# Two layers of an SSM and attention encoder: output projection in blocks of 512 columns, transposes of B and C at a fixed place

## The chip, the cores and the metric

The kernel runs on one core of a Trainium2 chip. The time is that of one execution on the device in microseconds (us), the median of several runs. The engines are TensorE (PE, matmuls; its weight loads are shown as PEld), VectorE (DVE), ScalarE (ACT), GpSimd (POOL) and SyncE (SP), which issues most of the DMA transfers.

## What is computed

A token matrix x of 256 rows and 2,048 columns goes through two layers. Cut to what matters:

```python
for l in range(DEPTH):                       # DEPTH = 2
    u, gate_ssm, q, k, v, gate_attn = split(h @ w_in[l])     # 2048 -> 6 x 1024
    y = s5_scan(u, ..., reverse=False) + s5_scan(u, ..., reverse=True) + d * u
    y = gelu(y); y = y * sigmoid(y @ w_glu[l] + b_glu[l])
    y = y * silu(gate_ssm)
    o = rms_norm(diff_attention(q, k, v, lam)) * (1 - lam_init) * silu(gate_attn)
    h = layer_norm(alpha * h + concat(y, o) @ w_out[l], ln_g[l], ln_b[l])
```

Here s5_scan is a complex diagonal state space model (SSM) over 64 groups of 16 channels with 64 states, run in both directions over the 256 tokens; B (64 x 16 for a group) maps the inputs to states, C maps states to outputs. diff_attention is softmax attention with two maps for each of 8 heads. All of it is in float32.

## The kernel before, in words

**Three products.** PE multiplies rounded float32 (fp32r). To keep float32's accuracy each operand is split into a high and a low part, and `mm3` (L167 to L170) issues high x high, high x low and low x high into one accumulator. A weight piece of 512 rows x 256 columns (512 KB) comes by one DMA of SP into one of 4 `raw` buffers (`load`, L143); `do_split` (L155) makes `wh` by a cast on ACT (L162) and `wl` by a subtraction on DVE (L164), two pieces ahead of their use. `step` (L829) takes the next piece of the list `jobs`, issues its matmuls, prepares the pieces behind it and then lets side work in. Almost all of PE's time is in these projections.

**The list of jobs.** For each layer: the input projection in blocks of 256 columns (4 pieces of 512 rows each, 24 blocks); the output projection's rows of the attention half (8 blocks of 256 columns, 2 pieces each: the first half, L942 to L951, put into `part_r` with the residual `xr` added); the projection of the GLU (4 blocks); the output projection's rows of the SSM half (the second half, L976 on). The last blocks of the second half (`late`: the last two of eight in layer 0 and the last three in layer 1) are interleaved by token halves with the LayerNorm that follows (`ln_finish`, L214). In the output projection the tokens are the weights of PE: one matmul has 128 rows of the token matrix as 128x128 weights and 256 columns of w_out as its moving operand. A block has two accumulators, one for each half of the tokens, in one PSUM bank.

**Side work.** The SSM and the attention heads are generators that run in lanes: after each step `side` (L778) lets the lanes go on as far as a budget allows; a `yield c, n` says what the piece cost and in how many steps it may go on. Lanes that the change touches or that its effects reach: `ssm_load` (L403 on; B and C are loaded, and PE transposes them, L421 and L446, 16 each a layer, with copies on ACT), `ssm_in` (U, the input of the SSM, times B, from L473 on), `ssm_scan`, and `ssm_out` (eight outputs `o`; for each of them on ACT a copy of states `bh`, L638, of taps `kw`, L570, and `lt`, L582; on PE L577 and the matmuls L586, L596 and L601 into `ss`; then ACT's copy `ub<-ss`, L607; at the end L626 applies gelu to `yT`, the SSM's output read back from memory, with a load of ACT's function table).

**What sets the order.** The code gives an order by its text and lanes; a scheduler then orders the instructions of each engine by a modelled timeline, with the waits that the data need. `after(ins)` pins an instruction behind another of the same engine. PSUM has eight banks: `acc` 2, `sc` one tile of 2 banks (the heads' scores, and later an accumulator of late blocks), `tp` 2, `ss` 2. In SBUF the tag `a8` has three buffers of 8 KB a partition, which pass from one tensor to the next: B's and C's sources in `ssm_load`, U, the heads' output oT, the SSM gates `sgs` (Silu of four gate blocks, L934), yT and the token operand of the second half.

Of the kernel before, what the change touches and what calls it, by code (L numbers as in the profile page):

```python
# [38 lines left out]
SCAN_COST = 1.0  # L39
HEAD_HOPS = (1,1,2,2,2,3)  # L40


@with_exitstack
def kernel(
# [80 lines left out]
    for l in range(DEPTH):  # L125
        for s in range(4):
            jobs += [(l, "in", 0, s), (l, "in", 1, s)]
        order = [2, 3]
        for hp in range(4):
            order += [8 + hp, 12 + hp, 16 + hp]  # L130
        order += list(range(20, 24)) + list(range(4, 8))
        for cb in order:
            jobs += [(l, "in", cb, s) for s in range(4)]
        for cb in range(8):
            jobs += [(l, "out", cb, 2), (l, "out", cb, 3)]
        for cb in range(4):
            jobs += [(l, "glu", cb, 0), (l, "glu", cb, 1)]
        for cb in range(8):
            jobs += [(l, "out", cb, 0), (l, "out", cb, 1)]
    raws, split = {}, {}  # L140
    newest = [None]

    def load(i):  # L143
        if i >= len(jobs):
            return
        l, kind, cb, s = jobs[i]
        src = {"in": w_in, "glu": w_glu, "out": w_out}[kind][l]
        raw = T([128, KT, 256], "raw", RAW_BUFS)
        newest[0] = SY.dma_start(
            raw,  # L150
            src[s * KT * 128:(s + 1) * KT * 128, cb * 256:(cb + 1) * 256].rearrange("(k p) c -> p k c", p=128),
        ).ins
        raws[i] = raw

    def do_split(i, wh=None, wl=None, behind=None):  # L155
# [3 lines left out]
        if wh is None:  # L159
            wh = T([128, KT, 256], "wh", SPLIT_AHEAD + 1, F32R)  # L160
            wl = T([128, KT, 256], "wl", SPLIT_AHEAD + 1, F32R)
        A.copy(wh, raw)  # L162
# [4 lines left out]
    def mm3(o, lh, ll, rh, rl, first, last):  # L167
        PE.matmul(o, lhsT=lh, rhs=rh, start=first, stop=False, skip_group_check=True)  # L168
        PE.matmul(o, lhsT=lh, rhs=rl, start=False, stop=False, skip_group_check=True)  # L169
        PE.matmul(o, lhsT=ll, rhs=rh, start=False, stop=last, skip_group_check=True)  # L170

# [231 lines left out]
    def ssm_load(l):  # L403
# [14 lines left out]
        for q in range(4):  # L418
            t = tp_bank([128, 4, 128])
            for c in range(4):  # L420
                PE.transpose(t[:, c, :], natv[:, :, 4 * q + c], ident)  # L421
            A.copy(Bv[:, :, 4 * q:4 * q + 4], t.rearrange("p c g -> p g c"))
# [17 lines left out]
        Cv = z.C.rearrange("p r (o g) c -> p r o (g c)", o=8)  # L440
        yield 0.0, 1
        for ri in range(2):
            for q in range(2):
                t = tp_bank([128, 4, 128])
                for o in range(4):
                    PE.transpose(t[:, o, :], cn[:, ri, 4 * q + o, :], ident)  # L446
                A.mul(Cv[:, ri, 4 * q:4 * q + 4, :], t, 1.0 if ri == 0 else -1.0)
# [390 lines left out]
    def acc_bank():  # L838
        return PS([128, 2, 256], "acc", 2)

    def sub_step(acc, s, hi, lo, k0, k1, tok_major=False, budget=BUDGET, k_outer=False):

# [22 lines left out]
    for l in range(DEPTH):  # L865
# [76 lines left out]
        part_r = [T([128, D], tag) for tag in ("xh1", "xl1")]  # L942
        for cb in range(8):
            cs = slice(cb * 256, (cb + 1) * 256)
            xr = T([128, 2, 256], "xr", 2)
            SY.dma_start(xr, xres[:, cs].rearrange("(i p) d -> p i d", p=128))
            acc = acc_bank()
            for s in (0, 1):
                sub_step(acc, s, M.hi, M.lo, 0, 7, tok_major=True)
            for i in range(2):  # L950
                V.scalar_tensor_tensor(part_r[i][:, cs], xr[:, i], ALPHA, acc[:, i, :], mult, add)  # L951
        finish(l_out)
# [22 lines left out]
        late = range(7 - len(places), 8)  # L975
        for cb in range(late[0]):  # L976
            if l + 1 < DEPTH and cb in (0, 2):
                with after(newest[0]):
                    next(l_load)
            cs = slice(cb * 256, (cb + 1) * 256)  # L980
            acc = acc_bank()
# [95 lines left out]
```

## Time and profile before

| | us |
|---|---|
| median of three runs | 1003.33 |
| lowest and highest of them | 999.39, 1005.35 |
| the profiled execution | 1002.55 |
| its span in the trace | 1000.8 |
| PE busy | 955.8 |
| DVE busy | 780.3 |
| ACT busy | 576.0 |
| POOL busy | 71.7 |

The mean granted clock of PE over the span is 0.991. The page of the profile gives the busy time of each engine; the timeline gives the instructions of a stretch with their start and length, and in square brackets how long the engine was idle before one and what released it; the waits say who waited for whom; the windows give busy time, granted clock and the share of the DMA engines for a stretch. A matmul's length goes from its start to its modelled end, and matmuls overlap, so a matmul's share in PE's time is read from the distance between starts.

### The profile page before, as it was taken

Reading aid. Unit: us, or ns where it says so; the run is one execution under the profiler, and the core shown is the slowest. Engines: PE = TensorE matmul, PEld = TensorE weight load, DVE = VectorE, ACT = ScalarE, POOL = GpSimd, SP = SyncE. Lnnn points to the kernel's source line nnn. Section 1 sums busy time; section 2 is a strip of 40 time slices with the busy share of each in tenths; the row PEclk is TensorE's granted clock in tenths of the full one; section 3 lists DMA queues with packets and bytes.
Section 4 is the critical chain, followed back from the end, with each engine's and each line's share of the span. In section 5 each row is a group of like instructions: output and inputs, shape, how many; then the busy total and the mean of one; then the engine's idle time right before and its main releaser. Section 6 shows DMA issues by size and latency. Waiting matters only on the chain.

```text
span 1000.8 us, 24625 instructions
## 1 busy us (share of the span) xinstructions
PE 955.8 (96%) x10304; PEld 926.8 (93%) x10304; DVE 780.3 (78%) x1353; ACT 576.0 (58%) x950; POOL 71.7 (7%) x103
## 2 busy tenths in 40 slices
PE   2999999999999998999979999999999999999995
PEld 2989988999999998999979989999999999999995
DVE  6875799899887786656588699899899759565676
ACT  2546588565575697545344585555556769843640
POOL 1000130210200000000011030010100100000001
PEclk9999999999999999999989999999999999999998
DMA  9898521545554643779875724555445454576953
GB/s 272 254 256 230 184 81 44 168 149 169 156 183 153 193 145 104 234 228 260 215 231 167 233 68 126 170 169 161 157 150 187 151 168 136 178 237 209 270 173 85
DMA packets 193167, 177.76 MB, mean 178 GB/s; under 512 B 37536, under 2 KB 185760, under 8 KB 193056
## 3 DMA queue, kind: packets, MB, share of 16 engines
q1 hardware_dynamic: 193056, 176.18, 58.7%
q8 instruction: 81, 1.33, 0.6%
q14 instruction: 30, 0.25, 0.1%
HBM read 165.02 MB, written 11.14 MB: 176 GB/s over the span
## 4 chain that ended last, share of the span: by engine, by line
PE 81%; DMA 7%; DVE 6%; ACT 3%; issue 1%; SPq 1%; POOL 0%; POOLq 0%; DVEq 0%; ACTq 0%
PE acc L168 23%; PE acc L169 23%; PE acc L170 23%; DMA raw<-in_w_out_dram 3%; PE ss L596 2%; DVE wl L164 2%; PE ss L501 1%; PE sc L707 1%; PE ss L735 1%; PE tp L473 1%; ACT wh L162 1%; PE tp L577 1%; DVE w L456 1%; DVE H L235 1%; DMA H<-in_x_dram 1%
## 5 line engine op out<-in xcount | busy, mean ns | idle before, releaser
L164 DVE TENSOR_TENSOR wl<-raw,wh 128x1024 fp32r<-128x1024 f32 x266 | 324.9, 1223 | 143.0 <-ACT wh L162 141.8
L162 ACT CAST wh<-raw 128x1024 fp32r<-128x1024 f32 x266 | 278.2, 1050 | 251.0 <-PE acc L169 118.7
L168 PE MATMUL acc<-xh,wh 128*128 128x256 f32 x1280 | 370.9, 290 | 0.8 <-ACT xh L252 0.5
L169 PE MATMUL acc<-xl,wh 128*128 128x256 f32 x1280 | 365.2, 286 | 0.8 <-DVE xl L253 0.7
L170 PE MATMUL acc<-xh,wl 128*128 128x256 f32 x1280 | 364.1, 285 | 1.1 <-DVE wl L164 1.1
L168 PEld LDWEIGHTS acc<-xh,wh 128*128 128x128 f32 x1280 | 245.5, 192 | 6.2 <-ACT xh L252 1.4
L169 PEld LDWEIGHTS acc<-xl,wh 128*128 128x128 f32 x1280 | 245.7, 192 | 2.4 <-DVE xl L253 1.5
L170 PEld LDWEIGHTS acc<-xh,wl 128*128 128x128 f32 x1280 | 245.6, 192 | 2.1 <-DVE wl L164 1.5
L168 PE MATMUL acc<-wh,xh 128*128 128x256 f32 x512 | 146.3, 286 | 0.0
L169 PE MATMUL acc<-wl,xh 128*128 128x256 f32 x512 | 145.4, 284 | 0.0
L170 PE MATMUL acc<-wh,xl 128*128 128x256 f32 x512 | 145.0, 283 | 0.0
L169 PEld LDWEIGHTS acc<-wl,xh 128*128 128x128 f32 x512 | 98.2, 192 | 0.2
L168 PEld LDWEIGHTS acc<-wh,xh 128*128 128x128 f32 x512 | 98.1, 192 | 0.1
L170 PEld LDWEIGHTS acc<-wh,xl 128*128 128x128 f32 x512 | 98.2, 192 | 0.0
L169 PE MATMUL acc<-wl,a 128*128 128x256 f32 x208 | 59.1, 286 | 2.1 <-DVE wl L164 2.1
L168 PE MATMUL acc<-wh,a 128*128 128x256 f32 x208 | 58.7, 284 | 0.0
L170 PE MATMUL acc<-wh,a 128*128 128x256 f32 x208 | 58.5, 283 | 0.0
L551 DVE TENSOR_TENSOR sa<-tab,H 128x256 f32<-128x256 f32 x126 | 53.0, 421 | 2.9 <-ACT H L504 0.7
L458 DVE TENSOR_TENSOR w<-w,x 128x512 f32<-128x512 f32 x64 | 45.6, 712 | 0.8
L169 PEld LDWEIGHTS acc<-wl,a 128*128 128x128 f32 x208 | 39.7, 191 | 3.3 <-DVE wl L164 3.3
L717 ACT ACTIVATE e<-sc,mx 128x256 f32<-128x256 f32 x64 | 29.5, 477 | 21.0 <-DVE mx L711 21.0
L168 PEld LDWEIGHTS acc<-wh,a 128*128 128x128 f32 x208 | 39.7, 191 | 0.4 <-ACT wh L162 0.4
(198 smaller groups left out, 1482.9 us busy)
## 6 DMA issues: line engine op xcount, KB each, us to landing
raw<-in_w_in_dram SPq DMA_DIRECT2D x192, 512.0 KB, 3.8
raw<-in_w_out_dram SPq DMA_DIRECT2D x64, 512.0 KB, 4.6
raw<-in_w_glu_dram SPq DMA_DIRECT2D x16, 512.0 KB, 4.4
xr<-xres SPq DMA_DIRECT2D x16, 256.0 KB, 4.3
xres<-H SPq DMA_DIRECT2D x14, 256.0 KB, 3.4
H<-in_x_dram SPq DMA_DIRECT2D x8, 256.0 KB, 5.9
u_dr<-ub SPq DMA_DIRECT2D x8, 256.0 KB, 3.3
a<-u_dr SPq DMA_DIRECT2D x8, 256.0 KB, 3.8
```

The source lines that it names most:

```text
L162: A.copy(wh, raw)
L164: V.tensor_tensor(wl, raw, wh.bitcast(F32), sub)
L168: PE.matmul(o, lhsT=lh, rhs=rh, start=first, stop=False, skip_group_check=True)
L169: PE.matmul(o, lhsT=lh, rhs=rl, start=False, stop=False, skip_group_check=True)
L170: PE.matmul(o, lhsT=ll, rhs=rh, start=False, stop=last, skip_group_check=True)
L235: last = V.scalar_tensor_tensor(r[:, i, cs], r[:, i, cs], rstd, bt[:, cs], mult, add)
L456: V.tensor_tensor(dst, t.unsqueeze(2).to_broadcast([128, 8, 16, 4]), M[:, m, gs, :].unsqueeze(3).to_broadcast([128, 8, 16, 4]), mult)
L458: V.tensor_tensor(w[:, r], w[:, r], x2, op)
L473: PE.transpose(t[:, pr, :], ws[o][:, ri, 2 * pr:2 * pr + 2].rearrange("p g c j -> p (g c j)"), ident)
L551: V.tensor_tensor(a.rearrange("p v q r g -> p v q (r g)"), lam, h.unsqueeze(1).to_broadcast([128, 2, 16, 8]), mult)
L596: PE.matmul(yps[d][halves[g2], pr, :], lhsT=w[halves[d], ri, g].rearrange("p c j -> p (c j)"), rhs=h[:, ::-1] if d else h, start=ri == 0, ...
L717: A.activation(e[:, m, i, :], sc[:, m, i, :], AF.Exp, bias=mx[:, c:c + 1], accum_out=sm[:, c:c + 1])
```

## The change

The output projection gets wide blocks of 512 columns. A wide block has four pieces of 256 rows x 512 columns (512 KB as before), two row tiles each, and two accumulators of one whole bank each. `wide_banks` takes the two `acc` banks for even blocks and the two banks of `sc` for odd ones. In the first half all blocks are wide (4 of 512 columns). In the second half `WIDE` gives the number: 3 in layer 0 and 2 in layer 1; the blocks behind them keep 256 columns. The residual `xr` is loaded as two tiles of 128 rows x 512 columns in place of one of 256 rows x 256 columns. `mm3` notes its last matmul in `newest[1]`, and each transpose of B and C is pinned behind the newest one. Before C's transposes the lane now pauses three steps in place of one. The code of the next layer's `ssm_load` is started at the first two wide blocks of the second half (before: at its blocks 0 and 2).

```diff
+WIDE = (3,2)
...
-        for cb in range(8):
-            jobs += [(l, "out", cb, 2), (l, "out", cb, 3)]
+        for cb in range(4):
+            jobs += [(l, "wide", cb, s) for s in range(4, 8)]
         for cb in range(4):
             jobs += [(l, "glu", cb, 0), (l, "glu", cb, 1)]
-        for cb in range(8):
+        for cb in range(WIDE[l]):
+            jobs += [(l, "wide", cb, s) for s in range(4)]
+        for cb in range(2 * WIDE[l], 8):
             jobs += [(l, "out", cb, 0), (l, "out", cb, 1)]
...
+    def shape_of(i):
+        return (2, 512) if jobs[i][1] == "wide" else (KT, 256)
...
-        raw = T([128, KT, 256], "raw", RAW_BUFS)
+        k, n = shape_of(i)
+        raw = T([128, k, n], "raw", RAW_BUFS)
...
-        PE.matmul(o, lhsT=ll, rhs=rh, start=False, stop=last, skip_group_check=True)
+        newest[1] = PE.matmul(o, lhsT=ll, rhs=rh, start=False, stop=last, skip_group_check=True).ins
...
-                PE.transpose(t[:, c, :], natv[:, :, 4 * q + c], ident)
+                with after(newest[1]):
+                    PE.transpose(t[:, c, :], natv[:, :, 4 * q + c], ident)
...
-        yield 0.0, 1
+        yield 0.0, 3
...
-                    PE.transpose(t[:, o, :], cn[:, ri, 4 * q + o, :], ident)
+                    with after(newest[1]):
+                        PE.transpose(t[:, o, :], cn[:, ri, 4 * q + o, :], ident)
...
+    def wide_banks(n):
+
+        if n % 2:
+            t = PS([128, 2, 512], "sc", 1)
+            return [t[:, i] for i in range(2)]
+        return [PS([128, 512], "acc", 2) for _ in range(2)]
+
+    def wide_block(n, s0, k0, k1):
+
+        accs = wide_banks(n)
+        for s in range(s0, s0 + 4):
+            def fn(wh, wl):
+                for i in range(2):
+                    ms = slice(128 * i, 128 * i + 128)
+                    for k in range(2):
+                        kt = 2 * s + k
+                        mm3(accs[i], M.hi(kt)[:, ms], M.lo(kt)[:, ms], wh[:, k, :], wl[:, k, :], kt == k0, kt == k1)
+            step(fn)
+        return accs
...
-        for cb in range(8):
-            cs = slice(cb * 256, (cb + 1) * 256)
-            xr = T([128, 2, 256], "xr", 2)
-            SY.dma_start(xr, xres[:, cs].rearrange("(i p) d -> p i d", p=128))
-            acc = acc_bank()
-            for s in (0, 1):
-                sub_step(acc, s, M.hi, M.lo, 0, 7, tok_major=True)
+        for cb in range(4):
+            cs = slice(cb * 512, (cb + 1) * 512)
+            xrs = []
             for i in range(2):
-                V.scalar_tensor_tensor(part_r[i][:, cs], xr[:, i], ALPHA, acc[:, i, :], mult, add)
+                xrs.append(T([128, 512], "xr", 2))
+                SY.dma_start(xrs[i], xres[128 * i:128 * i + 128, cs])
+            accs = wide_block(cb, 0, 0, 7)
+            for i in range(2):
+                V.scalar_tensor_tensor(part_r[i][:, cs], xrs[i], ALPHA, accs[i], mult, add)
...
-        for cb in range(late[0]):
-            if l + 1 < DEPTH and cb in (0, 2):
+        for cb in range(WIDE[l]):
+            if l + 1 < DEPTH and cb < 2:
                 with after(newest[0]):
                     next(l_load)
+            accs = wide_block(cb, 4, 8, 15)
+            cs = slice(cb * 512, (cb + 1) * 512)
+            for i in range(2):
+                V.tensor_tensor(r[:, i, cs], part_r[i][:, cs], accs[i], add)
+                for c in range(2):
+                    ln_stats(r, i, 2 * cb + c, st)
+        for cb in range(2 * WIDE[l], late[0]):
```

Line numbers of the changed program: mm3 is L175 to L177, ACT's cast L169, LayerNorm's transposes L255, the transposes of B and C L429 and L455, the taps L579 and L591, the output's copy L616, gelu L635, its cast L638, the states' copy L647, the gates' Silu L963.

The change also moves instructions that it does not name. On PE, at the border between the layers, where the last matmuls of layer 0's output projection (weights in `bh`) meet LayerNorm's transposes (L248) and layer 1's first projections (tokens in `xh`), there stood before:

```order
L248 MATMUL ss<-cst,H 128x128 x4
L170 MATMUL acc<-bh,a_5916 128x256
L248 MATMUL ss<-cst,H 128x128 x4
L421 MATMUL tp<-cst,a_6197 128x128 x8
L446 MATMUL tp<-cst,a_6986 128x128 x8
L248 MATMUL ss<-cst,H 128x128 x4
L168 MATMUL acc<-xh_6665,wh 128x256 x2
```

and now:

```order
L255 MATMUL ss<-cst,H 128x128 x4
L177 MATMUL acc<-bh,a_5714 128x256
L255 MATMUL ss<-cst,H 128x128 x8
L175 MATMUL acc<-xh_6312,wh 128x256 x2
L176 MATMUL acc<-xl_6313,wh 128x256
```

The eight transposes of B and the eight of C are gone from the border; they stand among layer 1's projections.

On ACT, in layer 1, at the end of the SSM outputs, `a8_10734` is sgs (the Silu of its gate blocks is L934), `acc_11172` its second gate block, and the last copy `ub<-ss_11446` that of the eighth output. Before:

```order
L934 ACTIVATE a8_10734<-acc_11172 128x512
L638 COPY bh_10770<-H_7266 128x1024
L607 COPY ub_11251<-ss_11280 128x256
L582 COPY lt0_72<-tp_11332 64x2x64 x4
L570 COPY kw_11396<-kx_7267 128x256 x2
L162 CAST wh_11600<-raw_11420 128x1024
L607 COPY ub_11393<-ss_11351 128x256
L582 COPY lt0_72<-tp_11403 64x2x64 x4
L607 COPY ub_11393<-ss_11446 128x256
L162 CAST wh_11630<-raw_11498 128x1024
L626 ACT_TABLE_LOAD
L626 ACTIVATE a8_11491<-a8_11491 128x512 x2
```

In the changed program `a8_10395` is sgs, `acc_10396` and `acc_11080` are its first two gate blocks, `a8_11076` is yT, and `ss_11031` is the eighth output. Around the sixth output's copy (`ss_10865`):

```order
L579 COPY kw_10910<-kx_6979 128x256 x2
L635 ACT_TABLE_LOAD
L635 ACTIVATE a8_11076<-a8_11076 128x512 x2
L169 CAST wh_11185<-raw_10934 128x1024
L647 COPY bh_10382<-H_6978 128x1024
L616 COPY ub_10836<-ss_10865 128x256
```

and from the seventh to the eighth:

```order
L169 CAST wh_11217<-raw_11085 128x1024
L616 COPY ub_11008<-ss_10966 128x256
L591 COPY lt0_72<-tp_11018 64x2x64 x4
L638 CAST bh_11141<-a8_11076 128x512 x2
L616 COPY ub_11008<-ss_11031 128x256
L963 ACT_TABLE_LOAD
L963 ACTIVATE a8_10395<-acc_10396 128x512
L963 ACTIVATE a8_10395<-acc_11080 128x512
L169 CAST wh_11247<-raw_11115 128x1024
```

The Silu of the first two gate blocks stands behind the eighth output's copy now, where that of the second stood ahead of the sixth's, and gelu with its table load stands ahead of the sixth output's copy, where it stood behind the eighth's. The buffers of the tag a8 have changed hands with it: in layer 1, by the addresses in the built programs, sgs took before a buffer that C's source had left, and yT the one that U had; in the changed program sgs has U's buffer and yT the other one. U is read by the matmuls of all eight outputs.

## Rows read from the trace of the kernel before

**Rows 1.** The first part of the profile's page: busy time, share and instructions of each engine.

```profile
PE 955.8 (96%) x10304; PEld 926.8 (93%) x10304; DVE 780.3 (78%) x1353; ACT 576.0 (58%) x950; POOL 71.7 (7%) x103
```

**Rows 2.** Timeline of PE at 428 us: start, length, engine, line, operation, tiles, shapes.

```profile
428.10 0.28 PE L168 MATMUL acc<-wh,xh 128*128 128x256 f32 x1
...
428.46 0.28 PE L168 MATMUL acc<-wh,xh 128*128 128x256 f32 x1
```

**Rows 3.** Timeline of PE at 525 us, at a granted clock of 0.5.

```profile
524.75 0.41 PE L170 MATMUL acc<-xh,wl 128*128 128x256 f32 x1
524.96 0.41 PE L168 MATMUL acc<-xh,wh 128*128 128x256 f32 x1
```

**Rows 4.** Timeline of PE in layer 0's SSM outputs; in brackets idle before, releaser.

```profile
388.56 0.50 PE L596 MATMUL ss<-bh,w 64*64 64x64 f32 x8 [2.85 <-ACT ub L607]
```

**Rows 5.** Timeline of PE at the border between the layers.

```profile
500.17 0.85 PE L421 MATMUL tp<-cst,a 128*128 128x128 f32 x6
...
515.51 1.20 PE L421 MATMUL tp<-cst,a 128*128 128x128 f32 x8
...
521.02 1.94 PE L446 MATMUL tp<-cst,a 128*128 128x128 f32 x8 [4.31 <-DMA a<-in_ssm_c_re_dram]
522.75 1.06 PE L248 MATMUL ss<-cst,H 128*128 128x128 f32 x4
...
523.91 0.80 PE L168 MATMUL acc<-xh,wh 128*128 128x256 f32 x2
```

**Rows 6.** Windows: columns as in the head line, one row for each stretch.

```profile
core 0: us, PE busy (x) PEld busy (x) DVE busy (x) ACT busy (x) POOL busy (x), PEclk, DMA share, GB/s
388.80:392.20 3.40, 3.40 (x87) 3.28 (x84) 2.36 (x4) 3.31 (x7) 0.00 (x0) 0.50 0.29 77
463.00:504.00 41.00, 39.11 (x315) 37.74 (x313) 25.39 (x38) 15.89 (x18) 0.00 (x0) 1.00 0.90 226
518.50:521.90 3.40, 0.88 (x5) 0.91 (x6) 2.86 (x7) 0.00 (x0) 1.14 (x2) 0.51 0.95 269
815.00:857.00 42.00, 42.00 (x939) 39.92 (x938) 33.50 (x51) 35.99 (x66) 0.00 (x0) 1.00 0.42 125
118.00:172.00 54.00, 52.70 (x1039) 46.55 (x1038) 46.76 (x76) 42.45 (x78) 10.31 (x14) 1.00 0.24 71
560.00:612.00 52.00, 51.79 (x1009) 46.68 (x1008) 41.19 (x61) 38.27 (x57) 8.25 (x11) 1.00 0.42 124
```

**Rows 7.** Timeline of PE at 262 us, in the attention heads.

```profile
262.55 1.05 PE L735 MATMUL ss<-v,wT 128*128 128x128 f32 x8
```

**Rows 8.** Waits from 455 to 505 us: who waited for whom: us, times, longest.

```profile
ACT wh L162 <- DMA raw<-in_w_out_dram: 13.6, 6, 4.1
...
PE acc L169 <- DVE wl L164: 1.9, 3, 0.9
```

**Rows 9.** Timeline of ACT in layer 1's SSM outputs.

```profile
836.67 0.37 ACT L607 COPY ub<-ss 128x256 f32<-128x256 f32 x1
...
839.96 2.21 ACT L638 COPY bh<-H 128x1024 f32<-128x1024 f32 x1 [0.18 <-PE ss L596]
842.20 0.37 ACT L607 COPY ub<-ss 128x256 f32<-128x256 f32 x1
842.47 1.11 ACT L582 COPY lt<-tp 64x128 f32<-64x128 f32 x4
843.61 0.77 ACT L570 COPY kw<-kx 128x256 f32<-128x256 f32 x2
844.29 1.04 ACT L162 CAST wh<-raw 128x1024 fp32r<-128x1024 f32 x1
845.35 0.60 ACT L934 ACTIVATE a<-acc 128x512 f32<-128x512 f32 x1
```

**Rows 10.** Timeline of ACT in layer 0, gelu and its table load.

```profile
383.75 1.28 ACT L626 ACT_TABLE_LOAD   x1 [1.33 <-DMA a<-y_dr]
385.04 1.15 ACT L626 ACTIVATE a<-a 128x512 f32<-128x512 f32 x2
```

More of the change, by code (lines that the diff above doesn't have):

```diff
@@ L133 @@
             jobs += [(l, "in", cb, s) for s in range(4)]
-        for cb in range(8):
-            jobs += [(l, "out", cb, 2), (l, "out", cb, 3)]
+        for cb in range(4):
+            jobs += [(l, "wide", cb, s) for s in range(4, 8)]
         for cb in range(4):
             jobs += [(l, "glu", cb, 0), (l, "glu", cb, 1)]
-        for cb in range(8):
+        for cb in range(WIDE[l]):
+            jobs += [(l, "wide", cb, s) for s in range(4)]
+        for cb in range(2 * WIDE[l], 8):
             jobs += [(l, "out", cb, 0), (l, "out", cb, 1)]
     raws, split = {}, {}
-    newest = [None]
+    newest = [None, None]
+    def shape_of(i):
+        return (2, 512) if jobs[i][1] == "wide" else (KT, 256)
     def load(i):
@@ L146, in load @@
         l, kind, cb, s = jobs[i]
-        src = {"in": w_in, "glu": w_glu, "out": w_out}[kind][l]
-        raw = T([128, KT, 256], "raw", RAW_BUFS)
+        src = {"in": w_in, "glu": w_glu, "out": w_out, "wide": w_out}[kind][l]
+        k, n = shape_of(i)
+        raw = T([128, k, n], "raw", RAW_BUFS)
         newest[0] = SY.dma_start(
             raw,
-            src[s * KT * 128:(s + 1) * KT * 128, cb * 256:(cb + 1) * 256].rearrange("(k p) c -> p k c", p=128),
+            src[s * k * 128:(s + 1) * k * 128, cb * n:(cb + 1) * n].rearrange("(k p) c -> p k c", p=128),
         ).ins
@@ L159, in do_split @@
         if wh is None:
-            wh = T([128, KT, 256], "wh", SPLIT_AHEAD + 1, F32R)
-            wl = T([128, KT, 256], "wl", SPLIT_AHEAD + 1, F32R)
+            wh = T([128, *shape_of(i)], "wh", SPLIT_AHEAD + 1, F32R)
+            wl = T([128, *shape_of(i)], "wl", SPLIT_AHEAD + 1, F32R)
         A.copy(wh, raw)
```

## The prediction

> **What bounds the kernel now.** I read the busy shares first [rows 1]: TensorE (PE) is busy for 955.8 of 1000.8 us, VectorE (DVE) for 780.3, ScalarE (ACT) for 576.0. So a microsecond counts if it shortens the matmul stream or takes away a wait of PE. In the projections PE waits for nothing. A matmul of the three-product scheme starts 0.36 us after the third before it, which is 0.120 us each for 256 columns [rows 2]; each comes with a weight load of its own. At half clock (granted 0.50, the 1.2 GHz level) the same matmul starts 0.21 us after the last [rows 3]; more exactly 256 columns at 1.2 per ns are 0.2133 us, with nothing over. At the 2.4 GHz level the columns alone would be 0.1067, so 0.0133 of each 0.120 us are not columns. That remainder is what wide matmuls can save.
>
> The other waits are short and known. At 388.6 PE waits 2.85 us for ACT, in the tail of the SSM outputs of layer 0 [rows 4]. At 521.0 it waits 4.31 us for the load of ssm_c, with transposes of C in front of LayerNorm's [rows 5]. At 463 to 504 the DMAs are 0.90 busy and PE is busy for 39.11 of 41 us [rows 6]. Layer 1 has no wait in its own tail of SSM outputs: PE is busy for all of 42 us from 815 to 857 [rows 6].
>
> **Part 1: wide matmuls.** In the first half of the output projection all of the 8 blocks become 4 wide ones in both layers; in the second half 6 blocks of 8 in layer 0 and 4 of 8 in layer 1. A block of 256 columns over 1,024 rows of w_out has 48 matmuls (8 row tiles, 2 token halves, 3 products). So 16 + 10 = 26 blocks x 48 = 1,248 matmuls become 624 of twice the columns. They take 1,248 x 0.120 = 149.8 us now. No row shows a matmul of 512 columns. Bounds from the nearest rows: 0.2133 us if only columns count (saves 16.6), 0.240 us if the 0.0133 is a property of the columns (saves nothing). Between them lies 0.2133 + 0.0133 = 0.2267 us, if the 0.0133 comes once per weight load: 624 x 0.2267 = 141.4, saves 8.3 us. I take this. Eight 128-column matmuls of another kind take 1.05 us together from the first start to the last end; if the last lasts 0.28 as one in [rows 2] does, they start (1.05 - 0.28) / 7 = 0.11 us apart, with a load of the same 128x128 weights in each [rows 7]. A weight load is thus not what needs 0.120 us by itself, and the remainder is more likely columns and load disturbing each other at full speed, once per pair.
>
> The Trainium skill, "TensorE: Matmul & The Clock Gate", section "Back-to-back issue gap", gives columns / 2.4 + 2.5 ns for a warm gap. For 256 columns that would be 0.109 us where [rows 2] have 0.120, so the trace does not bear it out here; for 512 it would be 0.216, and the saving some 15 us.
>
> The accumulators cost nothing by this: blocks alternate between the two acc banks and the two sc banks, the heads that use sc are finished before, and an eviction has a block of some 10.9 us to end in. The DVE and ACT work per column stays.
>
> **Part 2: what the faster stream runs into.** In layer 0's second half ACT waits 13.6 us for loads of w_out and PE 1.9 us for the split behind them [rows 8]. The 144 wide matmuls there would save 1.9 us; the bytes do not shrink, so I give half back: +1.0 (bounds 0 and 2.5).
>
> **Part 3: the transposes.** Before, 8 of B stand at 500 to 503 us (six of them in [rows 5]), where PE waits for a split anyway [rows 8], and 8 of B and 8 of C in the gap in front of layer 1 [rows 5]. Now all 32 of layer 1 stand among its projections, 24 of them moved out of idle time. At 0.11 us each [rows 7] and some 0.1 for each of 6 switches that is +3.2. In return LayerNorm's transposes no longer stand behind the 8 of C. PE was at half clock there [rows 6], C ran from 521.02 to 522.75, 1.7 us [rows 5]. The data of LayerNorm bind again soon after, and the first projections then run at half clock, so I count 1.2. The 4.31 us themselves are no gain: PE has only LayerNorm to wait for there. Net +2.0 (0 to +3). B also comes later, so layer 1's input part of the SSM is pressed together as layer 0's is: PE lost 54 - 52.70 = 1.3 us there against 52 - 51.79 = 0.2 in layer 1 [rows 6]; +1.0 (0 to 3).
>
> **Part 4: a buffer that changes hands in layer 1.** This is the largest loss, and the diff does not name it. Tag a8 has three buffers. Before, sgs (the SSM gates) took the buffer that C's source had left, and yT took the one of U after the last output. In the program built from the changed code it is the other way round: yT has the free buffer, sgs has U's. U is read until the last of the 8 SSM outputs. So the Silu of the first two gate blocks stands behind the eighth output on ACT, as the order shows; both acc banks are full, and the third gate block can't start. The two gelu calls of yT move in front of the sixth output's copy besides.
>
> From rows: one output takes 5.5 us on ACT (836.67 to 842.20), and ACT is full in it: 2.21 + 0.37 + 1.11 + 0.77 + 1.04 [rows 9]. PE is as full. (a) Gelu with its table load adds 1.28 + 1.15 = 2.4 us [rows 10], which the seventh output waits. (b) The eighth has no matmuls in front any more; it waits for the four L582 copies of 1.11 us behind its taps: +1.2. (c) Then the copy of 0.37, a table load of 1.28 and a Silu of 0.60 [rows 9, 10] before PE may go on: +2.3. Sum 5.9 us of waiting within some 10. Layer 0 shows what a wait like this does to the clock: after the 2.85 us PE ran for 3.4 us at 0.50 [rows 4, 6]. Half of such a stretch is lost, 1.7 us; between none and about three of them gives 0 to 4.6, I take 2.1. Part 4: +8.0 (5.9 to 10.5).
>
> In layer 0 the same buffers are as before. There the first wide block needs both acc banks, so its second half waits for the last Silu, behind gelu and a split: about 3 us in place of the 2.85. Zero (-1 to +2).
>
> **Sum.** -8.3 + 1.0 + 2.0 + 1.0 + 8.0 = +3.7. The profiled execution took 1002.55 us (span 1000.8), a little under the median of the three runs, 1003.33. So 1002.55 + 3.7 = 1006.3; I say 1006.
>
> **Rivals.**
> A. The weight load hides wholly: a wide matmul takes 0.2133. For it: the half-clock rows have no remainder at all, so loads can hide behind 0.2133 us of columns. Against: [rows 7]. The saving is 16.6, and PE outruns the loads more (2.5): -16.6 + 2.5 + 2.0 + 1.0 + 8.0 = -3.1, 999.5 us; 997.4 if the clock holds in Part 4. The skill's gap of 2.5 ns, named above, is a weaker form of this.
> B. Slower: at full speed PE takes in columns at 256 per 0.120 us whatever their number, so a wide matmul takes 0.240 and saves nothing. For it: the remainder vanishes at half clock, as a limit on columns per ns would too. Then the losses stand alone: 0 + 0 + 2.0 + 1.0 + 8.0 = +11, 1013.6 us. It decides from about 0.230 us per wide matmul on, where the saving falls under 6.2.
> C. Part 4 is not paid: the gate matmuls find a bank in time, PE waits as little as in rows 6. For it: the order leaves 24 matmuls before the seventh output, and ACT might catch up. -8.3 + 1.0 + 2.0 + 1.0 = -4.3, 998.3 us.
>
> **How the numbers follow.** Forecast 0.45 (1003 to 1009.5 by its own bounds), A 0.25, B 0.18, C 0.12. A measurement of this kernel tells from no change what is over 0.5%, 5 us: under 998.3 is faster, over 1008.3 slower. Faster: a third of A and over half of C, 0.16. Slower: most of B and a third of the forecast, 0.32. Same: 0.52. The range leaves out the upper half of B and the lowest ends of A and C: 997 to 1014.
>
> **What would show it.** In the profile after: the start-to-start time of L175 to L177 with 128x512 (0.213, 0.227 or 0.240) settles A and B. In layer 1, some 800 to 860 us in, a wait of PE before L605 for ACT L616 or L591, then one of the first matmul of the third gate block for ACT L963, and a granted clock of 0.5 around them, show Part 4; without them it is C. At the start of layer 1 no L455 (C) in front of L255. A wait of PE of more than 3 us anywhere else would make the prediction wrong in a way that I have not seen.

## The result, and the profile after

The changed kernel takes 1011.27 us, the median of 13 runs (1007.83 to 1015.79); the kernel before takes 1002.88 (13 runs, 999.39 to 1007.08). The ratio is 1.0087, 95% interval 1.0067 to 1.0107: 8.7 us slower, 6.7 to 10.7. The profiled execution took 1009.2 us (span 1007.4), 6.65 us over that of the kernel before; its mean granted clock is 0.987, where it was 0.991. The forecast, +3.7 us and 1006, lies below that interval; the time is inside the range of 997 to 1014. It is above the 1009.5 that the forecast had as its own upper bound, and above the 1008.3 from which the prediction called the outcome slower: it had given that a chance of 0.32, and 0.52 to no difference. The profiled execution is 2.1 us under the median of its kernel, so the stages below show less of the loss than the timed runs.

The first part of the page stands against [rows 1]: PE has 624 matmuls less, and is busy 3.5 us less, in a span that is 6.6 us longer.

```profile
span 1007.4 us, 23325 instructions
...
PE 952.3 (95%) x9680; PEld 897.9 (89%) x9680; DVE 778.1 (77%) x1327; ACT 577.5 (57%) x950; POOL 66.0 (7%) x103
```

Timeline of PE in a wide block (start, length, engine, line, tiles, shapes), against [rows 2]: with the six rows that are left out there are seven steps from the first start to the last, 1.59 us, 0.227 us each.

```profile
419.90 0.39 PE L177 MATMUL acc<-wh,xl 128*128 128x512 f32 x1
...
421.49 0.39 PE L176 MATMUL acc<-wl,xh 128*128 128x512 f32 x1
```

Timeline of PE at the end of layer 1's SSM outputs; in brackets the idle time before, and what ended it. Where [rows 6] had no wait of PE in 42 us, there are three now, of 1.05, 0.28 and 3.42 us. The last one ends with the Silu of the gates.

```profile
847.70 0.45 PE L605 MATMUL ss<-bh,w 64*64 64x64 f32 x8 [1.05 <-ACT ub L616]
...
848.65 0.69 PE L605 MATMUL ss<-bh,w 64*64 64x64 f32 x11 [0.28 <-DVE ub L617]
...
858.13 0.39 PE L175 MATMUL acc<-xh,wh 128*128 128x256 f32 x1 [3.42 <-ACT a L963]
```

Timeline of ACT there, against [rows 9]: gelu with its table load stands ahead of the sixth output, and behind the eighth output's copy at 855.80 come a table load and the two Silu calls that the third gate block waits for.

```profile
841.83 1.28 ACT L635 ACT_TABLE_LOAD   x1
843.12 1.15 ACT L635 ACTIVATE a<-a 128x512 f32<-128x512 f32 x2
...
845.11 2.14 ACT L647 COPY bh<-H 128x1024 f32<-128x1024 f32 x1
847.28 0.37 ACT L616 COPY ub<-ss 128x256 f32<-128x256 f32 x1
...
855.80 0.37 ACT L616 COPY ub<-ss 128x256 f32<-128x256 f32 x1
856.19 1.28 ACT L963 ACT_TABLE_LOAD   x1
857.48 1.09 ACT L963 ACTIVATE a<-acc 128x512 f32<-128x512 f32 x2
```

Windows of the changed kernel (busy time and instructions of PE, PEld, DVE, ACT and POOL, then PE's granted clock, DMA share, GB/s): two stretches at half clock, one right behind the first of these waits and one behind the last.

```profile
848.80:852.20 3.40, 3.40 (x84) 3.28 (x82) 2.73 (x4) 1.96 (x4) 0.00 (x0) 0.50 0.47 138
859.00:862.40 3.40, 3.40 (x18) 3.40 (x18) 0.00 (x0) 0.00 (x0) 0.00 (x0) 0.51 0.42 126
```

Where the 6.65 us are, by stages of the two profiled executions. A stage goes from the start of its first projection matmul to that of the next stage's, read from PE's timeline by counting columns; its work in the cracks (SSM, heads, transposes) is in it. The last 0.3 us lie ahead of the first of these matmuls.

| stage | before | after | difference |
|---|---|---|---|
| start, to 4 of 24 input blocks of layer 0 | 59.3 | 60.5 | +1.2 |
| layer 0's input blocks to the last four (SSM input part, heads) | 242.6 | 243.4 | +0.8 |
| last four input blocks (SSM outputs) and first half, layer 0 | 118.7 | 114.0 | -4.7 |
| GLU | 22.6 | 22.6 | 0 |
| second half of layer 0 and border | 60.6 | 57.1 | -3.5 |
| SSM input part, layer 1 | 151.8 | 157.2 | +5.4 |
| heads, layer 1 | 131.1 | 132.0 | +0.9 |
| last four input blocks (SSM outputs), layer 1 | 66.8 | 75.5 | +8.7 |
| first half, layer 1 | 46.1 | 43.5 | -2.5 |
| GLU, layer 1 | 22.6 | 22.6 | 0 |
| second half of layer 1, to the end | 58.5 | 58.5 | 0 |

Such a table is of one execution each. Kernels with the same order of instructions at the start differ there by 58.5 to 62.1 us, and the second half of layer 0 with narrow blocks, where loads decide, came out at 55.1 to 60.6 us in the kernel before and the experiments. So +1.2 in the first row says nothing, and verdicts below go by the timed runs.

### The profile page after: what moved, and what is told of

The parts are those of the page before. It is cut to its first block, busy times and chain, and to the rows that moved or that the text cites. A ratio compares the mean times of both kernels' runs of the same rounds, so it can differ in the third digit from the quotient of the medians.

```text
span 1007.4 us, 23325 instructions
## 1 busy us (share of the span) xinstructions
PE 952.3 (95%) x9680; PEld 897.9 (89%) x9680; DVE 778.1 (77%) x1327; ACT 577.5 (57%) x950; POOL 66.0 (7%) x103
## 4 chain that ended last, share of the span: by engine, by line
PE 73%; DVE 12%; ACT 5%; DMA 5%; issue 3%; SPq 1%; POOL 1%; POOLq 0%; DVEq 0%; ACTq 0%
PE acc L175 20%; PE acc L176 20%; PE acc L177 19%; DVE wl L171 2%; DMA raw<-in_w_out_dram 2%; PE sc L175 2%; PE sc L176 2%; PE sc L177 2%; DVE w L465 2%; PE ss L605 1%; ACT wh L169 1%; PE sc L716 1%; DVE w L467 1%; DVE x L465 1%; PE ss L744 1%
## 5 line engine op out<-in xcount | busy, mean ns | idle before, releaser
L169 ACT CAST wh<-raw 128x1024 fp32r<-128x1024 f32 x266 | 279.0, 1051 | 259.0 <-PE acc L176 128.5
L175 PE MATMUL acc<-xh,wh 128*128 128x256 f32 x1280 | 372.2, 291 | 4.2 <-ACT a L963 3.4
L177 PE MATMUL acc<-xh,wl 128*128 128x256 f32 x1280 | 365.4, 286 | 1.0 <-DVE wl L171 1.0
L175 PEld LDWEIGHTS acc<-xh,wh 128*128 128x128 f32 x1280 | 246.8, 193 | 9.2 <-ACT a L963 3.6
L177 PEld LDWEIGHTS acc<-xh,wl 128*128 128x128 f32 x1280 | 247.1, 193 | 2.0 <-DVE wl L171 1.4
L175 PE MATMUL acc<-wh,xh 128*128 128x256 f32 (+1 forms) x320 | 97.6, 310 | 1.1 <-ACT a L963 1.1
L177 PE MATMUL acc<-wh,xl 128*128 128x256 f32 (+1 forms) x320 | 97.6, 305 | 0.0
L176 PE MATMUL acc<-wl,xh 128*128 128x256 f32 (+1 forms) x320 | 97.6, 305 | 0.0
L175 PEld LDWEIGHTS acc<-wh,xh 128*128 128x128 f32 x320 | 61.0, 191 | 4.0 <-ACT a L963 1.5
L177 PEld LDWEIGHTS acc<-wh,xl 128*128 128x128 f32 x320 | 61.1, 191 | 2.5
L176 PEld LDWEIGHTS acc<-wl,xh 128*128 128x128 f32 x320 | 61.1, 191 | 2.4
L563 DVE TENSOR_TENSOR H<-sa 128x128 f32<-128x128 f32 x126 | 36.2, 288 | 2.1
L562 DVE TENSOR_TENSOR sa<-sa,H 128x128 f32<-128x128 f32 x126 | 36.1, 287 | 1.8
L647 ACT COPY bh<-H 128x1024 f32<-128x1024 f32 x16 | 34.8, 2194 | 3.1 <-PE ss L605 1.6
L177 PE MATMUL acc<-bh,wl 128*128 128x256 f32 x128 | 36.1, 282 | 0.0
```

What stands on the lines that cost most here:

```text
L177: newest[1] = PE.matmul(o, lhsT=ll, rhs=rh, start=False, stop=last, skip_group_check=True).ins
L562: V.tensor_tensor(a[:, 0], a[:, 0], nx, add)
L563: V.tensor_tensor(nx, a[:, 0], a[:, 1, :, ::-1, :], add)
L647: A.copy(hc, src)
```

## Experiments

**The buffers of layer 1.** Three runs. The first puts the gates into U's buffer in the kernel before:

```diff
-        sgs = T([128, 8, 256], "a8", 3)
+        sgs = T([128, 8, 256], "a8", 3) if l == 0 else z.U.rearrange("p a b -> p (a b)").rearrange("p (o t) -> p o t", o=8)
```

> The kernel before with one edit: in layer 1 the SSM gates (sgs) are written into U's buffer, as the changed program has them; blocks narrow, transposes where they were. Theory (the buffer is what layer 1's SSM outputs lost 8.7 us by): 1002.9 + 8.7 = 1011.6 us, from 1009 to 1014, with PE waiting some 3 to 4 us for the gates' Silu behind the eighth output. Rival (the wide blocks or the pinned transposes are what costs there, and the buffer came along): 1003 us within 2.

Measured: 1006.9 us, ratio 1.0045 (1.0028 to 1.0061), 4.5 us slower. That is less than the theory gave. The timeline of ACT tells why:

```profile
848.57 1.28 ACT L934 ACT_TABLE_LOAD   x1
849.87 0.60 ACT L934 ACTIVATE a<-acc 128x512 f32<-128x512 f32 x1
850.36 2.03 ACT L638 COPY bh<-H 128x1024 f32<-128x1024 f32 x1
...
860.19 0.37 ACT L607 COPY ub<-ss 128x256 f32<-128x256 f32 x1
```

The Silu of the second gate block ran at 849.87, ten microseconds ahead of the eighth output's copy at 860.19. My reading is that, as a view of U, a slice of the gates waits only for the outputs that read the same slice of U, while a buffer that the pool hands on waits for all of them. So the edit has gelu and Silu with their table loads between the outputs, and a wait of PE for the sixth output's copy behind them, but not the wait behind the eighth output. It shows the direction and a part of the price. Timeline of PE in that run:

```profile
852.72 0.45 PE L596 MATMUL ss<-bh,w 64*64 64x64 f32 x8 [2.71 <-ACT ub L607]
```

The second is the pins of the transposes and the pause alone, with narrow blocks:

```diff
-                PE.transpose(t[:, c, :], natv[:, :, 4 * q + c], ident)
+                with after(newest[1]):
+                    PE.transpose(t[:, c, :], natv[:, :, 4 * q + c], ident)
...
-        yield 0.0, 1
+        yield 0.0, 3
...
-                    PE.transpose(t[:, o, :], cn[:, ri, 4 * q + o, :], ident)
+                    with after(newest[1]):
+                        PE.transpose(t[:, o, :], cn[:, ri, 4 * q + o, :], ident)
```

> The kernel before with the pins of the transposes and the pause of three steps alone; blocks stay narrow. The program built from it has sgs in U's buffer in layer 1, as the changed kernel has. Theory (wide blocks only gain, by 8.2 us; everything else that was lost comes with the pins): 1011.3 + 8.2 = 1019.5 us, from 1016 to 1022. Rival (wide blocks bring losses of their own, by their two banks or their loads): nearer to 1011, since what they lose would be gone with them.

Measured: 1013.37 us, ratio 1.0112 (1.0076 to 1.0147; four runs). The program has the buffers changed round although no block is wide: it is the pins and the pause that did it, by the order that the scheduler found for them. Its stage of SSM outputs in layer 1 takes 75.3 us, as in the changed kernel. The time lies nearer to the rival, 2.5 us (give or take 4.0) above the changed kernel where the theory had 8.2: wide blocks seem to give less than their matmuls.

The third is the changed kernel with yT put into U's buffer, so that the gates have the free one:

```diff
-            z.yT = T([128, 8, 256], "a8", 3)
-            for n in range(2):
-                SY.dma_start(z.yT[:, 4 * n:4 * n + 4],
-                             y_dr[512 * n:512 * n + 512].rearrange("(o p) t -> p o t", p=128))
+            z.yT = T([128, 8, 256], "a8", 3) if l == 0 else z.U.rearrange("p a b -> p (a b)").rearrange("p (o t) -> p o t", o=8)
+            first = None
+            for n in (1, 0) if l else (0, 1):
+                with after(first if l else None):
+                    first = SY.dma_start(z.yT[:, 4 * n:4 * n + 4],
+                                         y_dr[512 * n:512 * n + 512].rearrange("(o p) t -> p o t", p=128)).ins
```

> The changed kernel with one edit: in layer 1 yT is put into U's buffer, its second half loaded first, so that the gates have the free buffer as in the kernel before. Theory: 1011.3 - 8.7 = 1002.6 us, from 1000 to 1005; no wait for the gates' Silu behind the eighth output. Rival (the loss in layer 1 is from the first wide block needing both accumulator banks at once): the loss stays, 1009 to 1012.

Measured: 1003.67 us, ratio 1.0012 (0.9989 to 1.0035). The theory holds, the rival is out: the first wide block is still there, and the stage falls from 75.5 to 67.7 us. Timeline of ACT, the same place: the Silu of the second gate block is ahead of the seventh output's copy, and gelu's table load behind the eighth's. In the kernel before the pool handed U's buffer to yT; here yT is a view of U, which may differ a little.

```profile
849.97 0.60 ACT L965 ACTIVATE a<-acc 128x512 f32<-128x512 f32 x1
850.46 0.37 ACT L616 COPY ub<-ss 128x256 f32<-128x256 f32 x1
...
854.45 0.37 ACT L616 COPY ub<-ss 128x256 f32<-128x256 f32 x1 [2.45 <-PE ss L610]
...
862.34 1.28 ACT L637 ACT_TABLE_LOAD   x1
```

**Wide blocks alone, and where they stand.** The changed kernel without pins and with the old pause, so the diff of the second run above, taken back:

```diff
-                with after(newest[1]):
-                    PE.transpose(t[:, c, :], natv[:, :, 4 * q + c], ident)
+                PE.transpose(t[:, c, :], natv[:, :, 4 * q + c], ident)
...
-        yield 0.0, 3
+        yield 0.0, 1
```

> The changed kernel without the pins and with the pause of one step as before: wide blocks alone. The program built from it has the gates in the free buffer. Theory: 1002.9 - 8.2 = 994.7 us, up to 998 if the loads of layer 0's second half hold it up. Rival (wide blocks have a cost of their own in the tails): 1000 or more.

Measured: 1003.85 us, ratio 1.0012 (0.9990 to 1.0034). My theory fell: 8.2 us of matmuls are gone, and no time is won. The next four tell where it goes; none of them has pins, and the pause is that of one step. Wide blocks in the first halves alone:

```diff
-WIDE = (3,2)
+WIDE = (0,0)
...
         for cb in range(2 * WIDE[l], late[0]):
+            if WIDE[l] == 0 and l + 1 < DEPTH and cb in (0, 2):
+                with after(newest[0]):
+                    next(l_load)
```

> Wide blocks in the first half of each layer's projection alone, narrow ones in the second half, no pins, pause of one step. Wide blocks alone in both halves came out at 1003.9 us, no better than narrow ones, though their matmuls take 8.2 us less. Theory (the gain is given back where loads or splits are late: all of it in the two second halves, some 2 us of 5 in the first ones): about 3 us under the kernel before, 999 us, from 997 to 1001. Rival (wide blocks give back everything wherever they stand): 1002 to 1004.

Measured: 996.81 us, ratio 0.9967 (0.9946 to 0.9987). The same program ran once more with the next group (its label is a leftover, nothing is pinned in it):

> Wide blocks in the first half of each layer alone, once more, the same program as the run that came out at 996.8 us, beside the others on this chip: if that was no accident of a few runs, 995 to 998.5 us, under the kernel before by 3 to 6 us. Rival: within 2 us of the kernel before.

Measured: 997.3 us, ratio 0.9967 (0.9952 to 0.9982). This beats both kernels, by 3.3 us and by some 12. With wide blocks in layer 1's second half as well:

```diff
-WIDE = (0,0)
+WIDE = (0,2)
```

> Wide blocks in both first halves and in layer 1's second half (2 of them), narrow in layer 0's second half; no pins. With first halves alone it was 996.8 us, with both second halves as well 1003.9. Theory (layer 0's second half, where the DMAs are full, is where wide blocks lose; layer 1's is neutral, since one wait for ACT's cast takes what its matmuls save): 996 to 998.5 us. Rival (any wide block in a second half costs): 999 to 1001.

Measured: 997.15 us, ratio 0.9964 (0.9947 to 0.9980): neutral, as the theory has it. And in layer 0's second half instead:

```diff
-WIDE = (0,0)
+WIDE = (3,0)
```

> Wide blocks in both first halves and in layer 0's second half (3 of them), narrow in layer 1's second half; no pins. Theory: all of the difference to both second halves wide is here, so 1002 to 1004 us, and the stage of layer 0's second half is longer than with narrow blocks. Rival: half of it, 999 to 1001.

Measured: 1002.16 us, ratio 1.0017 (1.0001 to 1.0033). Against the same kernel with narrow blocks there (0.9967) it is 5.0 us slower, give or take 2.2. So layer 0's second half is where wide blocks without pins lose all that the others win. PE's timeline of this run shows on what:

```profile
482.35 0.51 PE L175 MATMUL sc<-wh,a 128*128 128x512 f32 x1 [1.23 <-ACT wh L169]
487.87 1.33 PE L428 MATMUL tp<-cst,a 128*128 128x128 f32 x5 [5.01 <-DMA a<-in_ssm_b_im_dram]
...
489.42 0.63 PE L177 MATMUL sc<-wh,a 128*128 128x512 f32 x1
489.85 0.63 PE L175 MATMUL sc<-wh,a 128*128 128x512 f32 x1
```

PE waits 5.01 us for the load of B, whose transposes without pins stand in the middle of a wide block, and then runs at half clock, 0.43 us from start to start where it was 0.227. Windows over the same 41 us as in [rows 6], first this run, then the one with narrow blocks there: PE is busy for 34.70 and for 41.00 of them.

```profile
463.00:504.00 41.00, 34.70 (x147) 27.71 (x145) 21.07 (x27) 13.91 (x16) 0.00 (x0) 0.92 0.79 209
```

```profile
463.00:504.00 41.00, 41.00 (x344) 41.00 (x344) 28.13 (x44) 16.78 (x18) 0.00 (x0) 1.00 0.93 253
```

With pins, where B's transposes do not stand there, the profiles show no such loss: the stage takes 57.1 and 58.1 us with wide blocks, and 56.2, 58.5 and 58.8 with narrow ones.

**Is it the loads?** Wide blocks in both halves, no pins, yT in U's buffer, and the loads of B and C taken out of layer 0's second half:

```diff
-            if l + 1 < DEPTH and cb < 2:
-                with after(newest[0]):
-                    next(l_load)
...
-            SY.dma_start(nat[64 * ri:64 * ri + 64], src[l].rearrange("d g p c -> g d (p c)"))
+            with after(newest[0] if l else None):
+                SY.dma_start(nat[64 * ri:64 * ri + 64], src[l].rearrange("d g p c -> g d (p c)"))
```

> Wide blocks in both halves as in the run without pins, and the loads of layer 1's B and C taken out of layer 0's second half: they are issued among layer 1's first loads. yT is put in U's buffer so that the gates have the free one. Theory (the DMAs are what the second half of layer 0 waits for, with B and C among them): that stage falls from 61.6 us to 57 or less, since the waits for late pieces and for C's load go; the time is about 998 us. Rival (pieces of 512 columns are slow by themselves, or ACT's casts are late for another reason): the stage stays at 60 to 62 us, the time at 1002 to 1005.

Measured: 1000.33 us, ratio 0.9990 (0.9967 to 1.0012). The stage falls to 53.7 us, more than the theory asked for, with one wait of PE left in it, for an eviction (1.62 us, DVE at L1010). The window over the same 41 us has the DMAs at 0.68:

```profile
463.00:504.00 41.00, 39.38 (x213) 33.98 (x212) 28.80 (x41) 17.08 (x17) 1.35 (x2) 1.00 0.68 201
```

So wide pieces are not slow by themselves in this profile; with B and C among them they are. Two things go at once here, B's and C's share of the DMAs and the places of their transposes in PE's order, and the run does not tell them apart. The total is 2.2 us under that of the wide blocks alone, give or take 3.1, which is not clear of noise. Of what the stage gains, layer 1's SSM input part takes 6.1 us back: with B and C late it has 157.9 us in place of 151.8.

**The pins without the buffers,** with narrow blocks, once with the pause of three steps (the diff of the pins and that of yT above, on the kernel before) and once with one:

```diff
-        yield 0.0, 3
+        yield 0.0, 1
```

> The kernel before with the pins and the pause of three steps, blocks narrow, and yT put into U's buffer in layer 1, so that the gates have the free one: the pins without the change of buffers. With the change of buffers it was 1013.4 us. Theory (what the pins cost is mostly the buffers; the border between the layers gains what layer 1's start loses): 1013.4 - 8.5 = 1004.9 us, from 1002 to 1007. Rival (the buffers cost 4.8 us, as they did without pins): 1008 to 1010.

> The kernel before with the pins, but with the pause of one step before C's transposes as in the kernel before, blocks narrow, yT in U's buffer in layer 1. With the pause of three steps it was 1006.5 us. Theory (the pause, not the pins, lets the SSM's input part start later and costs 4 us in layer 1 and 1 in layer 0, while the pins take C's transposes out of the border between the layers): 1006.5 - 5 = 1001.5 us, from 1000 to 1003; the stage of layer 1's SSM input back to 72 to 73 us from 76.4. Rival (the pins themselves cost, as 24 transposes now stand in PE's busy time): 1004 to 1007, the stage stays at 76.

Measured: 1006.47 us with three steps, ratio 1.0063 (1.0035 to 1.0092); 1010.04 with one, ratio 1.0095 (1.0063 to 1.0126). My theory of the pause fell: layer 1's SSM input part takes 157 us with either (105.6 of it up to the point where it was 100.7 before). The pause isn't what costs there. That the second came out 3.2 us slower still is not clear of noise (give or take 4.3). Its profile has the difference in layer 1's SSM outputs (71.4 us in place of 66.6): on ACT gelu and Silu take turns, with a table load at each turn, and a cast that PE waits 1.98 us for stands behind them. The kernel before has such turns too (table loads at 857.48, 863.47 and 865.38 us), so that they are the cause is not shown. Timeline of ACT in that run, then of PE:

```profile
866.36 1.28 ACT L630 ACT_TABLE_LOAD   x1
870.40 1.15 ACT L630 ACTIVATE a<-a 128x512 f32<-128x512 f32 x2 [2.76 <-DMA a<-y_dr]
...
872.51 1.28 ACT L938 ACT_TABLE_LOAD   x1
...
875.44 1.28 ACT L630 ACT_TABLE_LOAD   x1
```

```profile
878.87 0.38 PE L168 MATMUL acc<-xh,wh 128*128 128x256 f32 x1 [1.98 <-ACT wh L162]
```

**The matmul by itself.** A program of nothing but matmuls, 96 in a row of each width, measured once:

```python
    def other(n, i):
        t = pp.tile([128, 512], F32, name="other", tag="other", bufs=2)
        for k in range(96):
            j = 128 * (k % 3)
            PE.matmul(t[:, 0:n], lhsT=wts[:, k % 4, j:j + 128], rhs=mov[:, k % 4, 0:n], start=k == 0, stop=k == 95, skip_group_check=True)
        return t
```

> Not the encoder: fp32r matmuls of 512, 384, 256, 192, 128 and 64 columns, 96 in a row of each, once with other weights each time and once with the same, with no other engine at work; all of the encoder is left out. Theory (columns at 2.4 per ns and 13.3 ns once per matmul with its weight load): 0.227, 0.173, 0.120, 0.093 us apart, and for 128 and 64 columns a floor near 0.11 if the weight load sets it. Rival (the remainder comes from the other engines' traffic in the encoder): 0.213, 0.160, 0.107 us. No difference between other and same weights is expected, as each matmul has its own load.

Timeline of PE (other: other weights each time; same: the same ones):

```profile
23.90 21.92 PE L94 MATMUL other<-mov,wts 128*128 128x512 f32 x96
45.66 21.92 PE L100 MATMUL same<-mov,wts 128*128 128x512 f32 x96
...
81.02 16.83 PE L94 MATMUL other<-mov,wts 128*128 128x384 f32 x96
97.68 16.80 PE L100 MATMUL same<-mov,wts 128*128 128x384 f32 x96
...
127.96 11.68 PE L94 MATMUL other<-mov,wts 128*128 128x256 f32 x96
139.47 11.68 PE L100 MATMUL same<-mov,wts 128*128 128x256 f32 x96
...
164.62 10.86 PE L94 MATMUL other<-mov,wts 128*128 128x192 f32 x96
175.32 10.88 PE L100 MATMUL same<-mov,wts 128*128 128x192 f32 x96
...
199.68 10.83 PE L94 MATMUL other<-mov,wts 128*128 128x128 f32 x96
210.34 10.88 PE L100 MATMUL same<-mov,wts 128*128 128x128 f32 x96
...
234.78 17.51 PE L94 MATMUL other<-mov,wts 128*128 128x64 f32 x96
```

From start to start of the rows, by 96: 21.76 / 96 = 0.2267 us for 512 columns, 16.66 / 96 = 0.1735 for 384, 11.51 / 96 = 0.1199 for 256, and 0.111 for 192 and for 128. At 256, 384 and 512 columns it is 0.013 us over the columns, with no other engine at work, and the same with other weights as with the same ones. Below that there is a floor of 0.111, already at 192 columns, for which 0.093 was expected.

## Why the prediction held, and by which steps

**What carries the sum.** Four programs on the way from before to after give the parts by timed runs: before; pins alone, with the buffers as before (1.0063); with wide blocks (1.0012); with the buffers changed round (1.0087, the changed kernel). The pins cost 6.3 us (3.5 to 9.2), wide blocks on top of them give 5.1 back (give or take 3.7), the buffers cost 7.5 (give or take 3.0). Forecast were +3.0, -7.3 and +8.0. The signs were right; the sum was 5 us short, 3.3 of it at the pins and 2.2 at the wide blocks, each inside what its runs can tell or near it. The parts hold for this order of steps: without pins wide blocks bring nothing (1.0012 against 1), and with narrow blocks the buffers cost 4.9, give or take 4.6. The prediction said that a wait of PE of more than 3 us in a place that it does not name would make it wrong in a way that it had not seen. There is one, of 3.34 us, where it had a term of 1.0 for smaller ones (Part 2).

**Part 1, the price of a wide matmul: right.** 0.2267 was forecast; 0.227 is measured in the kernel and 0.2267 by itself. Rivals A (0.2133) and B (0.240) are out. The Trainium skill ("TensorE: Matmul & The Clock Gate", section "Back-to-back issue gap") gives columns / 2.4 + 2.5 ns for a warm gap, and calls the formula that of an isolated matmul. By estimate from it 512 columns would take 0.216 and 192 would take 0.083; the rows have 0.227 and 0.111, so these runs do not bear it out. That the remainder is columns and load disturbing each other is still an argument; shown is that it comes once per matmul and doesn't need other engines.

**Part 2, what the faster stream runs into: the step that was sized wrong in kind.** I took one surcharge of 1.0 for DMA waits in layer 0's second half. The term for this and the matmuls together, -7.3, came out at -5.1 with pins (give or take 3.7) and at nothing without them. In the changed kernel the wait is there, 3.3 us for a piece that comes late, with a stretch of 3.4 us at half clock behind it (waits and timeline of PE):

```profile
PE acc L175 <- ACT wh L169: 3.3, 1, 3.3
```

```profile
497.28 0.55 PE L175 MATMUL acc<-wh,a 128*128 128x256 f32 x1 [3.34 <-ACT wh L169]
497.63 0.41 PE L176 MATMUL acc<-wl,a 128*128 128x256 f32 x1
```

And the two parts of the change are not independent, as my sum had them. Without pins, B's transposes hold a place in PE's order that wide blocks reach before B's load has come, and wide blocks there cost 5 us. The pins take that wait away, so a part of what they cost is earned back there. Two more places give back what wide matmuls save, and I had neither: in layer 1's second half the matmuls save 1.3 us and the stage doesn't shorten; and without pins layer 1's SSM outputs and first half together gain 1.2 to 2.0 us, and 0.5 in the run with the late loads, where the matmuls save 2.5.

**Part 3, the transposes: right places, low by a part.** LayerNorm binds at the border at once, as said: in place of C it is DVE's H that PE waits for, 4.89 us where it was 4.31 [rows 5], and the first projections run at half clock again. Timeline of PE after:

```profile
516.78 0.66 PE L255 MATMUL ss<-cst,H 128*128 128x128 f32 x2 [4.89 <-DVE H L242]
...
518.98 0.42 PE L177 MATMUL acc<-xh,wl 128*128 128x256 f32 x1
519.20 0.42 PE L175 MATMUL acc<-xh,wh 128*128 128x256 f32 x1
```

Layer 1's SSM input part lost 5.4 us, where 3.2 for transposes and 1.0 for crowding were counted. Windows of that part, before and after:

```profile
523.90:675.70 151.80, 151.58 (x1871) 145.72 (x1872) 131.54 (x220) 89.48 (x142) 15.86 (x23) 1.00 0.51 156
518.00:675.30 157.30, 156.21 (x1898) 149.75 (x1896) 128.66 (x213) 92.05 (x148) 15.21 (x23) 0.99 0.51 155
```

PE is busy for 4.6 of the 5.4 us. The trace has the 24 transposes more that were counted on (107 matmuls of 128 columns into `tp` in place of the 83), and half clock for 3.1 us at the part's start in place of 1.5 (the stretch at the border goes to 521.1, where the part starts at 518.0; before to 525.4, start at 523.9), by estimate 0.8 us of loss, which the sum had not. It needs the place of the transposes and not the pin as such: the run with late loads has no pins, the same 24 transposes more, and 157.9 us, of which 1.4 are a wait for B's load. In layer 0 the pins hold too, and I counted nothing there; the profiles tell nothing of it, 242.7 to 243.4 us with pins where those without have 242.4 to 244.7. The profiled execution with pins and narrow blocks has a span 3.9 us longer than that of before (1004.7), near the 3.0; the timed runs say 6.3, at least 3.5. Of that gap 1.4 us is the profiled execution of before, which at 1002.55 lies above the median of the 19 runs of its kernel beside this one (1001.15). What makes up the rest is open: it isn't the pause, and no single stage of the profile has it.

**Part 4, the buffer: right, in mechanism and in its sum.** The stage lost 8.7 us against 8.0, and the runs give 7.5. Inside it the sizes were off against each other. The waits are 1.05 + 0.28 + 3.42 = 4.8 us in place of 5.9: gelu's is 1.05 where I had 2.4, the rest 3.7 where I had 3.5; half clock costs, by estimate, half of two stretches of 3.4, so 3.4 in place of 2.1. That these errors cancel is luck. Rival C is out. The diff doesn't name the buffers, and the experiment with pins alone shows that not even the wide blocks are needed for it.

**Layer 0's tail** was forecast at zero (1 us gained to 2 lost); with its first half it gained 2.1 us beyond the matmuls in the changed kernel. The wait of 2.85 us and its half clock [rows 4, 6] are gone, and one of 1.10 us for a Silu stands in their place. It was 1.3 us in the other kernel that has pins and wide blocks both; the rest show from 0.9 gained to 0.8 lost beyond their matmuls. Why it takes both is open, and with one execution each it may be chance.

## What to carry to other kernels

Before believing a diff, read from the built program which buffers a pool hands to whom: here an order pinned in one place turned two buffers round in another, and that cost as much as the change proper could win. Shorten matmuls where PE waits for nothing, and leave them where loads set the pace: the same wide blocks won 3.3 us in the first halves and, without pins, lost 5 in a second half that the DMAs fill. An instruction that stands early in an engine's order because the engine was slow becomes a wait when the engine gets faster.

## What the runs showed of the hardware

A matmul of this kernel's projections, in fp32r with 128x128 weights, takes 0.013 us beyond its columns at the 2.4 GHz level (0.2267, 0.1735 and 0.1199 us for 512, 384 and 256 columns), and 0.111 us for 192 columns and for 128. At the 1.2 GHz level nothing is over that the rows show: [rows 3] have 0.21 for 256 columns, the row pair at 489.42 us above 0.43 for 512.

The clock fell in one place where PE was shown waiting for nothing. In the program of matmuls alone, in its one run, it was full for all widths down to 128 columns, and fell during the matmuls of 64 columns, which began at 234.78; windows of that run:

```profile
12.80:230.00 217.20, 217.20 (x1289) 196.82 (x1288) 0.00 (x0) 6.99 (x15) 0.00 (x0) 1.00 0.00 1
235.00:238.00 3.00, 3.00 (x29) 3.00 (x28) 0.00 (x0) 0.59 (x1) 0.00 (x0) 1.00 0.00 0
240.00:274.00 34.00, 34.00 (x157) 33.72 (x157) 0.00 (x0) 0.43 (x2) 0.00 (x0) 0.50 0.00 0
```

PE is shown busy for all of 34.00 us at a granted clock of 0.50; what it did before, at a clock of 1.00, was to start a matmul of 64 columns every 0.11 us (29 in 3.00 us, two of them begun earlier). In layer 1's SSM outputs of the changed kernel the low clock followed waits of 1.05 and 0.28 us, and one of 3.42; by estimate it cost 1.7 us behind each, so as much again as some of the waits. The wait of 1.10 us in layer 0's tail had no low clock behind it.
